# Five changes to the order of work in a hybrid decoder step: query copies, decay tiles, transposes, small loads, first output weights

## The chip, the core and the metric

The kernel runs on one core of a Trainium2 chip. Its engines each work through a queue of their own in order: TensorE (PE: matmuls and transposes; PEld is its weight load), VectorE (DVE), ScalarE (ACT), GpSimd (POOL), and SyncE (SP), which issues nearly all transfers (DMAs). Engines wait for one another by semaphores. The metric is device time in microseconds (us) of one execution, lower is better.

## The reference

One layer of a decoder for a prompt of 1024 tokens (with 16 learned meta tokens ahead of it) and, beside it, 8 sequences that decode 4 tokens each over 1024 cached ones:

```python
h = rms_norm(x, norm_pre_g[l])
(q, k, v), sg, (gq, gk, gv, gf), gg = branch_inputs(h, w_in[l], w_alpha[l], b_alpha[l])
o_sb = sb_prompt(q, k, v, sb_bias[l])
o_gla, s_end = gla_prompt(gq, gk, gv, gf)
x = x + rms_norm(branch_output(o_sb, sg, o_gla, gg, gla_norm_g[l], w_out[l]), norm_post_g[l])
...
log_f = jax.nn.log_sigmoid((ga @ w_alpha + b_alpha).astype(jnp.float32)) / GLA_TAU
...
sp = jnp.where(mask, jax.nn.softplus(z), 0.0)
later = lax.cumsum(sp, axis=z.ndim - 1, reverse=True) - sp
return jnp.where(mask, jnp.exp(jax.nn.log_sigmoid(z) - later), 0.0)
...
S_new = (jnp.exp(b_last[:, :, 0, :])[..., None] * S
         + jnp.einsum('bhsk,bhsv->bhkv', k * jnp.exp(b_last - b), v))
...
mixed = jnp.concatenate([o_sb * jax.nn.silu(sg), o_gla * jax.nn.silu(gg)], axis=-1)
return mixed @ w_out
```

`sb_*` is stick-breaking attention (8 heads of 128), `gla_*` gated linear attention (4 heads, keys of 128, values of 256, chunks of 64). The decoding tokens do the same with keys and values from pages of a cache, found by a page table, and with a stored GLA state. The new keys, values and states are outputs too.

## The kernel before

Everything is f32; each product is made of three matmuls of a high and a low part (`wh`, `wl` of the weights, `hh`, `hl` of the activations). `ident`, `ntri`, `nones` are constant matrices.

An in-projection (`inproj`) makes 128 columns of `h @ w_in` for all 1072 tokens: eight weight blocks of 256 rows (SP loads `wr`, ACT casts it to `wh` in L184, DVE makes `wl` in L185), and for each block three token chunks of up to 384 (`acc_*_0` to `_2`, three PSUM banks) of six matmuls (L289 to L291). After each chunk it calls `W.beat()`. The Weaver `W` holds generators that do all other work: each beat advances those that are due, and `yield n` puts a generator off by n beats. A unit is thus 24 beats. A scheduler then sets each engine's order by priorities and dependences; `urgent()` raises priority for weights and evacuations, and `spread(ins)` ties an instruction's place (without a wait) to the last matmul issued, `W.mark`.

Staging buffers of 128x384 (`stage(...)`, pool `stg`) are seven in rotation.

The stages, one after the other on PE:

- Norms and transposes of x; then eight attention heads. A head projects v, k and q, one unit each. `ev_q` evacuates a query chunk: ACT writes the high part scaled (L620), DVE the low part from PSUM (L621), ACT the sample queries `qsm`. `load_v` reads back the values (`vr`, a DMA) and casts them to V (ACT L483, DVE L484). `attend` runs tiles with their exponentials (X, Y, hi_s; L490, L512) woven into the next head's units.
- `low_rank` (acc_ga, L315), then gates 0 to 2. `gate_group` evacuates a gate chunk: ACT copies `gx` (L438); DVE and ACT turn it into silu in `gs` (DVE L424, ACT L425 and L426, DVE L427, ACT L428, DVE L429); DVE multiplies it with the attention output `go` (L430); SP writes it to `md` in DRAM (L431).
- Four GLA heads: units gk, gq, gv_0, gv_1. `decay` makes the gates' logs (loads `walr` in L720, cast in L731, matmul `al` in L740). `level_masks` makes seven masks. `by_token` transposes keys and values (`tr_k`, `tr_v`, L868, evacuated in L870 and L873); `packed` transposes the sample rows (`trp_k`, `trp_v`, L857) into `pk` and `pv` (ACT L858, DVE L860). All these transposes use one PSUM bank. `chunks` then runs U (L930) and o per pair of chunks. A GLA head waits for its `kd` by `while "kd" not in res: W.beat()`.
- Gates 3 and 4; then gates 5 to 13, with the sample decoding: `z_feed` has made key products of the cached pages all along (`jk`, DVE L384, each fed by a page `kp`, 64 KB, SP), two beats a page, from the first head on. After its last page follow the masked sum `zm` (L1064), `spb` (L1087), `new_keys` (matmul Cs, L1105, and Cn), `chain` for each sequence (scan, matmuls C, L1133 to L1136) and `paged_values` (dO).
- Gates 14 and 15: `load_small` fetches the sample columns of the gates from `md` (L1206).
- The output projection, from seven products of combined 512-column blocks: `weights` loads `wr`, ACT casts into `ring` (L1315), DVE the low part (L1316); `split` makes the forms `f` (L1265); the matmuls are L1452 to L1454 into `b`.

## Time and profile before

| | us |
|---|---|
| median of three runs | 2154.19 (2152.64 to 2156.18) |
| the profiled execution | 2153.79 |
| its span in the trace | 2152.1 |
| PE busy in it | 2078.1 |
| DVE busy | 1572.5 |
| ACT busy | 993.1 |

The granted clock of PE was 0.991 of full speed over the span. Lines of the profile name the engine, the source line (L12 is line 12 of the kernel), the operation and out<-in by the program's names. A timeline row gives start, duration, engine, line and operation, and in brackets how long the engine had been idle and what ended that. In the view of waits a row gives who waited, for whom, how long in all, how often, and the longest.

### The profile page before, as it was taken

To read this page: it belongs to the slowest core of one execution; us is meant where nothing else is said; L and a number is where in the kernel's file an instruction comes from. 1 tells how busy PE (TensorE), PEld (TensorE's weight loads), DVE (VectorE), ACT (ScalarE), POOL (GpSimd) and SP (SyncE) were. 2 spreads that over 40 slices of the span, in tenths; PEclk is the share of its full clock that TensorE was granted. 3 is DMA by queue.
4 is the path that set the end of the run, shared out by engine and by line. 5 is a ranking of instruction groups with operands and counts; after the bars stand their busy time and mean duration, and the time that the engine had idled before them with its cause. 6 is when DMAs were issued, how large, how long until landed. Compare 5 with 4: busy or idle time off the path is not lost.

```text
span 2152.1 us, 43331 instructions
## 1 busy us (share of the span) xinstructions
PE 2078.1 (97%) x12546; PEld 1872.8 (87%) x12546; DVE 1572.5 (73%) x6592; ACT 993.1 (46%) x2536; POOL 83.2 (4%) x298
## 2 busy tenths in 40 slices
PE   5999999999999999999999999999999999999997
PEld 5999999998999979998899898998788887777765
DVE  6368889888898879788788887977544347453575
ACT  7345556564655546432534435343443336332342
POOL 0000010000000010020000000000000000000000
PEclk9999999999999999999999999999999999999999
DMA  6125554554555453442343434335776766452485
GB/s 196 52 70 137 139 158 134 161 146 140 149 152 157 135 142 113 124 100 75 107 106 84 117 80 112 97 83 138 221 228 221 222 200 210 130 158 76 128 277 178
DMA packets 380802, 304.02 MB, mean 141 GB/s; under 512 B 50770, under 2 KB 321042, under 8 KB 380562
## 3 DMA queue, kind: packets, MB, share of 16 engines
q1 hardware_dynamic: 378370, 300.97, 48.0%
q8 instruction: 99, 1.62, 0.3%
q14 instruction: 141, 1.16, 0.2%
q10 hardware_dynamic: 2192, 0.27, 0.1%
HBM read 243.39 MB, written 57.72 MB: 140 GB/s over the span
## 4 chain that ended last, share of the span: by engine, by line
PE 71%; DVE 12%; DMA 10%; ACT 3%; issue 3%; SPq 1%; POOL 0%; DVEq 0%; ACTq 0%; POOLq 0%
DVE jk L384 5%; PE acc_g L289 4%; PE acc_g L291 4%; PE acc_g L290 4%; PE b L1452 4%; PE b L1453 4%; PE b L1454 4%; DMA kp<-in_cache_k_dram 3%; PE acc_k L289 3%; PE acc_k L290 3%; PE acc_k L291 3%; PE acc_gv L289 2%; PE acc_gv L291 2%; PE acc_gv L290 2%; PE acc_q L289 2%
## 5 line engine op out<-in xcount | busy, mean ns | idle before, releaser
L384 DVE SCALAR_TENSOR_TENSOR jk<-kp,qb 128x128 f32<-128x128 f32 x2048 | 590.5, 288 | 90.2 <-DMA kp<-in_cache_k_dram 51.8
L289 PE MATMUL acc_g<-hT,wh_g 128*128 128x304 f32 (+2 forms) x768 | 253.8, 330 | 5.1 <-ACT gx L438 4.7
L291 PE MATMUL acc_g<-hT,wl_g 128*128 128x368 f32 (+2 forms) x768 | 248.0, 323 | 0.0
L290 PE MATMUL acc_g<-hT,wh_g 128*128 128x304 f32 (+2 forms) x768 | 247.9, 323 | 0.0
L289 PEld LDWEIGHTS acc_g<-hT,wh_g 128*128 128x128 f32 x768 | 144.9, 189 | 31.9 <-ACT wh_g L184 12.1
L1452 PE MATMUL b<-ring,f 128*128 128x512 f32 x416 | 165.8, 400 | 3.4 <-ACT b L1351 1.6
L1316 DVE TENSOR_TENSOR ring<-wr,ring 128x512 fp32r<-128x512 f32 x104 | 70.6, 689 | 133.0 <-ACT ring L1315 132.5
L384 DVE DVE_READ_ACCUMULATOR jk<-kp,qb 128x1 f32 x2048 | 166.1, 81 | 0.1
L1453 PE MATMUL b<-ring,f 128*128 128x512 f32 x416 | 162.5, 391 | 0.7 <-DVE ring L1316 0.7
L1454 PE MATMUL b<-ring,f 128*128 128x512 f32 x416 | 162.2, 390 | 0.0
L291 PEld LDWEIGHTS acc_g<-hT,wl_g 128*128 128x128 f32 x768 | 145.0, 189 | 1.6 <-issue 1.6
L290 PEld LDWEIGHTS acc_g<-hT,wh_g 128*128 128x128 f32 x768 | 145.1, 189 | 0.7
L1315 ACT CAST ring<-wr 128x512 fp32r<-128x512 f32 x104 | 64.0, 621 | 162.9 <-DMA wr<-in_w_out_dram 80.9
L512 ACT ACTIVATE X<-X 127x512 f32<-127x512 f32 (+4 forms) x112 | 54.9, 491 | 165.2 <-DVE X L511 165.1
L289 PE MATMUL acc_gv<-hT,wh_gv 128*128 128x384 f32 (+1 forms) x384 | 130.1, 339 | 0.0
L289 PE MATMUL acc_k<-hT,wh_k 128*128 128x378 f32 (+1 forms) x384 | 127.6, 332 | 0.0
L291 PE MATMUL acc_gv<-hT,wl_gv 128*128 128x384 f32 (+1 forms) x384 | 126.0, 328 | 0.0
L289 PE MATMUL acc_q<-hT,wh_q 128*128 128x368 f32 (+2 forms) x384 | 125.4, 326 | 0.0
L290 PE MATMUL acc_k<-hT,wh_k 128*128 128x378 f32 (+1 forms) x384 | 125.4, 326 | 0.0
L291 PE MATMUL acc_k<-hT,wl_k 128*128 128x378 f32 (+1 forms) x384 | 125.2, 326 | 0.0
L290 PE MATMUL acc_gv<-hT,wh_gv 128*128 128x384 f32 (+1 forms) x384 | 125.2, 326 | 0.0
L290 PE MATMUL acc_q<-hT,wh_q 128*128 128x368 f32 (+2 forms) x384 | 123.6, 322 | 0.0
(427 smaller groups left out, 5483.4 us busy)
## 6 DMA issues: line engine op xcount, KB each, us to landing
kp<-in_cache_k_dram SPq DMA_DIRECT2D x512, 64.0 KB
vr<-in_cache_v_dram SPq DMA_DIRECT2D x64, 512.0 KB
qb<-qsd SPq DMA_DIRECT2D x64, 256.0 KB
tf<-in_w_out_dram SPq DMA_DIRECT2D x64, 256.0 KB
td<-tf SPq DMA_DIRECT2D x64, 256.0 KB
wr_g<-in_w_in_dram SPq DMA_DIRECT2D x128, 128.0 KB
wr<-td SPq DMA_DIRECT2D x64, 256.0 KB
wr<-in_w_out_dram SPq DMA_DIRECT2D x48, 256.0 KB
```

The costliest lines, as they stand in the source:

```text
L289: mm(acc[c][:, :n], wh[:, k2, :], hh[k][:, lo:hi], start=(k == 0), stop=False)
L290: mm(acc[c][:, :n], wh[:, k2, :], hl[k][:, lo:hi], start=False, stop=False)
L291: W.mark = mm(acc[c][:, :n], wl[:, k2, :], hh[k][:, lo:hi], start=False, stop=(k == NK - 1)).ins
L384: ins = vec.scalar_tensor_tensor(jk[:], kp[:], 1.0, qbs[h, b][:, t, :], ALU.mult, ALU.mult, accum_out=zt[:, t, NPG - 1 - i:NPG - i])
L512: act.activation(X, X, AF.Exp)
L1315: act.copy(wh, r)
L1316: vec.tensor_tensor(wl, r, wh.bitcast(F32), ALU.subtract)
L1452: mm(bk[:], ah, wh, start=first and k == 0, stop=False, skip_group_check=True)
L1453: mm(bk[:], ah, wl, start=False, stop=False, skip_group_check=True)
L1454: mm(bk[:], al, wh, start=False, stop=last and k == 7, skip_group_check=True)
```

## The change

Line numbers move by 21 to 28: L438 becomes L459, L620 becomes L641 and L646, L857 becomes L881, L860 L884, L868 L892, L930 L955, L1105 L1130.

- Queries: ACT copies each chunk to a staging buffer `qraw`, and a generator splits it from there.
- Decay: `walr` is loaded by one transfer that repeats its rows, for head 0 already during gate 2; the seven masks lie in one tile `lv` in place of seven staging buffers.
- Transposes: the keys' three groups are put two beats apart, `packed` of the keys comes last, and `packed` of the values two beats later.
- `new_keys` waits 16 beats in place of 10, `chain` 10 in place of 8.
- `load_small` is tied to the last matmul issued.
- The first four output weights' casts are tied each to an earlier chunk's matmul: `W.past` keeps the marks, and `spread` takes one from further back.

```diff
+                W.past.append(W.mark)
...
+    def load_ga(g, c):
+        lo, hi = CHUNKS[c]
+        gas[c] = stg.tile([96, 384], F32R, tag="stg", name=f"ga{g}_{c}")
+        nc.sync.dma_start(gas[c][:, :hi - lo].bitcast(F32), gad[:, lo:hi])
+
+    def decay_loads(g):
+        walr[g] = stage(f"walr{g}")[:96, :P]
+        a = w_alpha[0, :, g * P:(g + 1) * P]
+        nc.sync.dma_start(walr[g], bass.AP(tensor=a.tensor, offset=a.offset, ap=[[0, 6]] + [list(d) for d in a.ap]))
+        load_ga(g, 0)
...
-    def spread(ins):
+    def spread(ins, back=0):
         if W.mark is not None:
-            tc.add_manual_dep(ins.ins, W.mark.name, NOSYNC, reason="spread")
+            tc.add_manual_dep(ins.ins, (W.past[-1 - back] if back else W.mark).name, NOSYNC, reason="spread")
...
             def ev_q(c, ps, lo, hi):
                 e = min(hi, REAL)
-                a, b_, n = lo - META, e - META, e - lo
-                act.activation(qt[0][:, a:b_], ps[:, :n], AF.Copy, scale=QSCALE)
-                vec.scalar_tensor_tensor(qt[1][:, a:b_], ps[:, :n], QSCALE, qt[0][:, a:b_].bitcast(F32), ALU.mult, ALU.subtract)
-                if hi > REAL:
-                    act.activation(qsm[:], ps[:, n:], AF.Copy, scale=QSCALE)
-                    W.spawn(sample_q(h, qsm, ks), 5)
+                raw = stage(f"qraw{h}_{c}")
+                act.activation(raw[:, :hi - lo], ps, AF.Copy, scale=QSCALE)
+                W.spawn(split_q(raw, lo - META, e - META, hi - lo))
+
+            def split_q(raw, a, b_, w):
+                n = b_ - a
+                act.copy(qt[0][:, a:b_], raw[:, :n])
+                vec.tensor_tensor(qt[1][:, a:b_], raw[:, :n], qt[0][:, a:b_].bitcast(F32), ALU.subtract)
+                if w > n:
+                    act.copy(qsm[:], raw[:, n:w])
+                    W.spawn(sample_q(h, qsm, ks), 4)
...
         for g in range(3):
+            if g == 2:
+                W.spawn(first_decay_loads(), 14)
             gate_group(g)
...
-            for m in (64, 32, 16, 8, 4, 2, 1):
+            lv = xtile("lv")
+            for i, m in enumerate((64, 32, 16, 8, 4, 2, 1)):
-                a = stage(f"lv{m}")[:, :P]
+                a = lv[:, i * P:(i + 1) * P]
...
-            for i in range(6):
-                nc.sync.dma_start(raw[16 * i:16 * i + 16], w_alpha[0, :, g * P:(g + 1) * P])
+            if g:
+                decay_loads(g)
+            raw = walr.pop(g)
...
+            by_token(kt, kd, (0, 4), col, f"k{g}")
+            yield 2
+            by_token(kt, kd, (4, 4), col, f"k{g}")
+            yield 2
+            by_token(kt, kd, (8, 1), col, f"k{g}")
+            yield 2
             packed(rep_, pk[:], 2, f"k{g}")
-            by_token(kt, kd, (0, 4), col, f"k{g}")
-            yield 1
-            by_token(kt, kd, (4, 4), col, f"k{g}")
-            yield 1
-            by_token(kt, kd, (8, 1), col, f"k{g}")
...
             if c == 2:
+                yield 2
                 packed(rep, pv[:, f * P:(f + 1) * P], 1, f"v{g}_{f}")
...
         def new_keys():
-            yield 10
+            yield 16
...
             ch, cl = split_(s[:].rearrange("p a r -> p r a"), [P, NPG, 32], P, "dc", f"dc{b}")
-            yield 8
+            yield 10
...
-            nc.sync.dma_start(small[c][:, k, :], md[8 * c + k][:, SEQ:TOUT])
+            spread(nc.sync.dma_start(small[c][:, k, :], md[8 * c + k][:, SEQ:TOUT]))
...
-                act.copy(wh, r)
-                vec.tensor_tensor(wl, r, wh.bitcast(F32), ALU.subtract)
+                i = act.copy(wh, r)
+                j = vec.tensor_tensor(wl, r, wh.bitcast(F32), ALU.subtract)
+                if (p, q) == (1, 0) and k < 4:
+                    spread(i, 5 - k)
+                    spread(j, 5 - k)
```

How this moves instructions, at three places. First ACT at the end of the last head's query unit (`acc_q` is the query's accumulator, V the values, `wh_g` a weight of the next unit but one). Before:

```order
L483 CAST V_7_13958<-vr_0_13969 127x384
L544 COPY ost_0_13875<-O_0_13498 128x512
L184 CAST wh_g_1_14440<-wr_g_1_14438 128x256
L483 CAST V_7_13958<-vr_1_14000 127x384
L620 ACTIVATE q_7_13385<-acc_q_0_13388 128x368
L620 ACTIVATE q_7_13385<-acc_q_1_13389 128x384
L184 CAST wh_g_2_14510<-wr_g_2_14508 128x256
L620 ACTIVATE q_7_13385<-acc_q_2_13390 128x272
```

And now:

```order
L641 ACTIVATE qraw_0_13960<-acc_q_0_13430 128x368
L646 CAST q_7_13427<-qraw_0_13960 128x368
L641 ACTIVATE qraw_1_13970<-acc_q_1_13431 128x384
L646 CAST q_7_13427<-qraw_1_13970 128x384
L641 ACTIVATE qraw_2_14000<-acc_q_2_13432 128x304
L184 CAST wh_g_2_14558<-wr_g_2_14556 128x256
L646 CAST q_7_13427<-qraw_2_14000 128x272
L649 COPY qsm_13429<-qraw_2_14000 128x32
L504 CAST V_7_14006<-vr_0_14017 127x384
L533 ACTIVATE X_1_8_14057<-X_1_8_14057 33x32
L504 CAST V_7_14006<-vr_1_14048 127x384
```

The V casts moved from ahead of the query copies to behind them, among the first tiles' exponentials.

Second, ACT after gate 2, whose chunks are `gx_0` to `gx_2`, while PE begins the first GLA unit (`gk`). Before:

```order
L438 COPY gx_0_15982<-acc_g_0_15579 128x368
L425 ACTIVATE gs_16_15986<-gs_16_15986 128x368
L438 COPY gx_1_16001<-acc_g_1_15580 128x384
L426 ACTIVATE gs_16_15986<-gs_16_15986 128x368
L438 COPY gx_2_16039<-acc_g_2_15581 128x304
```

And now:

```order
L459 COPY gx_0_16034<-acc_g_0_15627 128x368
L446 ACTIVATE gs_16_16038<-gs_16_16038 128x368
L459 COPY gx_1_16053<-acc_g_1_15628 128x384
L447 ACTIVATE gs_16_16038<-gs_16_16038 128x368
L184 CAST wh_gk_2_16241<-wr_gk_2_16239 128x256
L446 ACTIVATE gs_384_16076<-gs_384_16076 128x384
L449 ACTIVATE gs_16_16038<-gs_16_16038 128x368
L447 ACTIVATE gs_384_16076<-gs_384_16076 128x384
L459 COPY gx_2_16091<-acc_g_2_15629 128x304
```

The copy of the third chunk moved four places back: its staging buffer is now the first chunk's.

Third, PE in the first GLA head, at the end of its last value unit and the start of the next unit. Before, `trp_k` stood ahead of the keys' transposes:

```order
L857 MATMUL trp_k_18062<-ident,rep_k_17917 96x128
L289 MATMUL acc_gv_1_1_17579<-hT_161,wh_gv_1_7_18047 128x384
L290 MATMUL acc_gv_1_1_17579<-hT_161,wh_gv_1_7_18047 128x384
L291 MATMUL acc_gv_1_1_17579<-hT_161,wl_gv_1_7_18048 128x384
L289 MATMUL acc_gv_1_1_17579<-hT_162,wh_gv_1_7_18047 128x384
L290 MATMUL acc_gv_1_1_17579<-hT_162,wh_gv_1_7_18047 128x384
L291 MATMUL acc_gv_1_1_17579<-hT_162,wl_gv_1_7_18048 128x384
L868 MATMUL tr_k_0_18066<-ident,gk_16075 128x128 x4
```

Now it stands behind the second `trp_v` and the first U:

```order
L881 MATMUL trp_v_1_18208<-ident,rep_v_1_18143 96x128
L289 MATMUL acc_gk_0_18218<-hT_150,wh_gk_1_18292 128x384
L290 MATMUL acc_gk_0_18218<-hT_150,wh_gk_1_18292 128x384
L291 MATMUL acc_gk_0_18218<-hT_150,wl_gk_1_18293 128x384
L955 MATMUL U_0_18304<-gv_0_17100,kd_18097 128x128
L955 MATMUL U_0_18304<-gv_1_17614,kd_18097 128x128
L881 MATMUL trp_k_18212<-ident,rep_k_17954 96x128
```

The DVE step that frees the bank for it, `pv`, stands now behind these rows (before, the split of `wal` came after it):

```order
L405 SCALAR_TENSOR_TENSOR jk_5_6_0_18246,zt_5_18005<-kp_5_6_18161,qb_5_17898 128x128
L405 SCALAR_TENSOR_TENSOR jk_5_6_1_18248,zt_5_18005<-kp_5_6_18161,qb_5_17898 128x128
L185 TENSOR_TENSOR wl_gk_3_18483<-wr_gk_3_18480,wh_gk_3_18482 128x256
L405 SCALAR_TENSOR_TENSOR jk_5_6_2_18250,zt_5_18005<-kp_5_6_18161,qb_5_17898 128x128
L755 TENSOR_TENSOR wal_18383<-walr_18254,wal_18383 32x128
L884 TENSOR_TENSOR pv_17099<-trp_v_1_18208,pv_17099 32x128
```

`trp_k` moved behind `pv`, and `pv` behind one more page of key products (`kp_5_6`) and `wal`.

More of the change, by code (lines that the diff above doesn't have):

```diff
@@ L55, in __init__ @@
     def __init__(self):
-        self.now, self.n, self.live, self.heap, self.mark = 0, 0, 0, [], None
+        self.now, self.n, self.live, self.heap, self.mark, self.past = 0, 0, 0, [], None, []
     def spawn(self, gen, delay=0, lasting=False):
@@ L326, in low_rank, with first_decay_loads @@
                     nc.sync.dma_start(gad[32 * i:32 * i + 32, lo:hi], t[:, :n].bitcast(F32))
+    gas, walr = {}, {}
+    def load_ga(g, c):
[7 more added lines that the diff above has]
+        load_ga(g, 0)
+    def first_decay_loads():
+        decay_loads(0)
+        return
+        yield
     dk_cm = tc.tile_pool(name="dk", bufs=2, side="right")
@@ L618, in ev_q @@
                 e = min(hi, REAL)
-                a, b_, n = lo - META, e - META, e - lo
-                act.activation(qt[0][:, a:b_], ps[:, :n], AF.Copy, scale=QSCALE)
-                vec.scalar_tensor_tensor(qt[1][:, a:b_], ps[:, :n], QSCALE, qt[0][:, a:b_].bitcast(F32), ALU.mult, ALU.subtract)
-                if hi > REAL:
-                    act.activation(qsm[:], ps[:, n:], AF.Copy, scale=QSCALE)
-                    W.spawn(sample_q(h, qsm, ks), 5)
+                raw = stage(f"qraw{h}_{c}")
[8 more added lines that the diff above has]
+                    W.spawn(sample_q(h, qsm, ks), 4)
+                return
+                yield
             inproj(C_SQ + h * P, ev_q, META, f"q{h}")
@@ L716, in decay @@
         def decay(g, cb):
-            raw = stage(f"walr{g}")[:96, :P]
-            for i in range(6):
-                nc.sync.dma_start(raw[16 * i:16 * i + 16], w_alpha[0, :, g * P:(g + 1) * P])
-            gas = {}
-            def load_ga(c):
-                lo, hi = CHUNKS[c]
-                gas[c] = stg.tile([96, 384], F32R, tag="stg", name=f"ga{g}_{c}")
-                nc.sync.dma_start(gas[c][:, :hi - lo].bitcast(F32), gad[:, lo:hi])
-            load_ga(0)
+            if g:
+                decay_loads(g)
+            raw = walr.pop(g)
             yield 6
@@ L737, in decay @@
                 if c < 2:
-                    load_ga(c + 1)
+                    load_ga(g, c + 1)
                 ps = gps.tile([P, 512], F32, tag="P", bufs=2, name=f"al{g}_{c}")
```

## The prediction

> **What bounds the kernel now.** I read the page's busy shares first, then the tensor engine's waits, then the clock in short windows, and last the timeline at each wait that the change touches. TensorE (PE) is busy almost throughout:

> ```profile
> span 2152.1 us, 43331 instructions
> ...
> PE 2078.1 (97%) x12546; PEld 1872.8 (87%) x12546; DVE 1572.5 (73%) x6592; ACT 993.1 (46%) x2536; POOL 83.2 (4%) x298
> ```

> The 74 us in which PE is not busy, and the time in which it runs at half clock, are all that a change of order can win; its matmuls stay. The view of waits says who held PE up (in all, times, longest, in us):

> ```profile
> PE acc_g L289 <- ACT gx L438: 4.7, 2, 2.4
> ...
> PE acc_ga L315 <- DVE q L621: 3.5, 1, 3.5
> PE trp_v L857 <- ACT gv L873: 3.1, 1, 3.1
> ...
> PE tr_k L868 <- DVE pk L860: 3.0, 4, 0.7
> ...
> PE al L740 <- DMA kp<-in_cache_k_dram: 2.7, 1, 2.7
> PE acc_v L289 <- DVE q L621: 2.7, 3, 1.5
> ...
> PE Cs L1105 <- issue: 1.6, 1, 1.6
> ...
> PE b L1452 <- ACT gx L438: 1.0, 2, 0.7
> PE b L1452 <- ACT ring L1315: 0.8, 2, 0.5
> ```

> The windows view adds a price that the waits don't show. Its columns are length, then busy time (with instructions) of PE, PEld, DVE, ACT, POOL, then the granted clock, the DMA share and GB/s:

> ```profile
> 791.00:794.50 3.50, 1.93 (x6) 0.87 (x7) 3.17 (x14) 1.66 (x6) 0.00 (x0) 0.53 0.26 72
> 794.50:798.00 3.50, 3.50 (x16) 2.14 (x15) 2.89 (x18) 1.33 (x6) 0.21 (x1) 0.50 0.80 244
> 798.00:801.50 3.50, 3.50 (x24) 2.33 (x23) 3.06 (x15) 1.03 (x4) 0.00 (x0) 0.99 0.10 27
> ...
> 1511.30:1515.00 3.70, 3.70 (x14) 3.23 (x14) 2.66 (x7) 1.57 (x4) 0.00 (x0) 0.54 0.65 237
> 1515.00:1518.00 3.00, 3.00 (x22) 3.00 (x21) 1.13 (x3) 2.46 (x6) 0.00 (x0) 1.00 0.99 312
> ...
> 1528.00:1531.80 3.80, 2.20 (x12) 1.57 (x11) 2.85 (x6) 1.38 (x2) 0.00 (x0) 1.00 0.78 243
> 1531.80:1535.30 3.50, 3.50 (x15) 1.61 (x15) 0.84 (x2) 1.08 (x2) 0.00 (x0) 0.52 0.34 126
> ```

> After a wait the clock stands near 0.5 for one stretch. At 1531.8 fifteen matmuls take 3.50 us; at the rate of 1515 to 1518 (22 in 3.0) they take 2.05, so the stretch cost 1.45. At 1511.3, 14 take 3.70 in place of 1.91: 1.8. I take 1.4 a stretch, since some of those matmuls are of odd shapes. After 791 there are two stretches: 22 matmuls in 5.43 busy us, which at the rate of 798 to 801.5 (24 in 3.5) take 3.2: 2.2.

> [...]

> **The change, part by part.**

> *Queries.* In each of eight heads ScalarE (ACT) now copies the accumulator out at once, and a split from SBUF follows. Before:

> ```profile
> 790.75 0.51 ACT L483 CAST V<-vr 127x384 fp32r<-127x384 f32 x1 [4.23 <-DMA vr<-out_dram]
> 791.16 0.85 ACT L620 ACTIVATE q<-acc_q 128x368 fp32r<-128x368 f32 x2
> ...
> 791.98 0.53 DVE L621 SCALAR_TENSOR_TENSOR q<-acc_q,q 128x368 fp32r<-128x368 f32 x1
> ```

> ACT stood 4.23 us before a cast that waited for a load, with the query behind it, and PE behind VectorE's (DVE's) half of the query. Now the raw copies come ahead of those casts, and no DVE step lies before the release. Removed: 3.5 + 2.7 + 2.2 of clock = 8.4. Added: 24 copies of some 0.45 us (0.85 for two), on an engine 46% busy: nothing, as long as the V casts behind them don't hold it. Those casts still wait for their loads, now in front of the first attention tiles' exponentials and of a weight cast. The nearest row is the 4.23 us above; PE reaches that weight two blocks of 18 matmuls later, 5.3 us at the rate of 798, so I take 1.4 in all (0 to 4.2). Net -7.0 (-8.4 to -4.2).

> *Decay tiles and masks.* The alpha weights come as one transfer during the third gate unit instead of six later, the masks in one tile. That removes the 2.7 us wait of `al` and one stretch: -4.1. But the two loads hold two of the seven staging buffers, and the copy of the third gate chunk now gets the buffer of the first, which DVE still reads (L429). Rows:

> ```profile
> 906.49 0.40 ACT L438 COPY gx<-acc_g 128x304 f32<-128x304 f32 x1
> ...
> 907.45 0.46 PE L289 MATMUL acc_gk<-hT,wh_gk 128*128 128x304 f32 x1
> ...
> 908.50 0.29 DVE L384 SCALAR_TENSOR_TENSOR jk<-kp,qb 128x128 f32<-128x128 f32 x1 [3.23 <-DMA kp<-in_cache_k_dram]
> ...
> 911.53 0.53 DVE L429 TENSOR_TENSOR gs<-gs,gx 128x368 f32<-128x368 f32 x1
> ...
> 919.84 0.30 ACT L731 CAST wal<-walr 96x128 fp32r<-96x128 f32 x1 [3.33 <-DMA walr<-in_w_alpha_dram]
> ```

> PE uses that bank at 907.45, and DVE frees the buffer at 912.06: with 0.4 for the copy, 5.0 of wait at most. In the new order of SP's queue the page of keys that held DVE 3.23 us no longer stands behind the 256 KB query block, so I take half, +2.5 (0 to 5.0, and 1.4 if the clock falls). Net -1.6 (-4.1 to +2.3).

> *trp_v, 3.1 us and a stretch.* ACT's order there is unchanged; long exponentials of the masks' stage stand ahead of the `gv` copies that PE awaits, and they ran late. The decay work now starts some 50 DVE instructions earlier. Even odds: -2.2 (-4.5 to 0).

> *Transposes spaced*, in four GLA heads:

> ```profile
> 1018.74 0.27 PE L857 MATMUL trp_k<-ident,rep_k 128*96 128x128 f32 x1
> 1020.80 0.66 PE L868 MATMUL tr_k<-ident,gk 128*128 128x128 f32 x4 [0.74 <-DVE pk L860]
> ...
> 1027.52 0.32 PE L857 MATMUL trp_v<-ident,rep_v 128*96 128x128 f32 x1
> ...
> 1028.36 0.61 PE L930 MATMUL U<-gv,kd 128*128 128x128 f32 x4
> ...
> 1027.76 0.29 DVE L384 SCALAR_TENSOR_TENSOR jk<-kp,qb 128x128 f32<-128x128 f32 x1 [2.05 <-DMA kp<-in_cache_k_dram]
> ...
> 1029.10 0.28 DVE L860 TENSOR_TENSOR pv<-trp_v,pv 32x128 fp32r<-32x128 f32 x1
> ...
> 1030.69 0.28 DVE L732 TENSOR_TENSOR wal<-walr,wal 32x128 fp32r<-32x128 f32 x1 [0.98 <-ACT wal L731]
> ```

> All these transposes share one PSUM bank, so each waits until the one before is read. `trp_k` no longer stands before `tr_k`: -3.0. It now follows `trp_v` after three accumulating matmuls and the two U: about 1.1 us (0.84 to U with four, one fewer, and 0.45 for U). But `pv` ended 1.86 us after `trp_v` started, behind a wait for keys; and the split of `wal` and one more group of key products now stand ahead of it in three heads. With an idle DVE nothing is lost; at 1.86 it is 0.8; behind `wal` (1030.97) and `pv`, 2.6. I take 1.2: +4.8 (0 to 10.4). Net +1.8 (-3.0 to +7.4). The longer wait for `kd` adds some five beats without matmuls per head, so the key products run about 20 beats earlier in the program by the fifth gate unit.

> *New keys, chain.* Because of those beats the sample stage starts a gate unit's worth earlier, and Cs stands 20 PE instructions earlier in spite of its longer delay:

> ```profile
> 1510.30 0.41 DVE L1087 TENSOR_TENSOR spb<-spn,bmask 32x256 f32<-32x256 f32 x1
> ...
> 1506.85 0.60 DVE L1064 TENSOR_TENSOR zm<-znall,bmask 32x256 f32<-32x256 f32 x1 [0.82 <-DMA znall<-znd]
> ...
> 1490.92 0.51 ACT L425 ACTIVATE gs<-gs 128x368 f32<-128x368 f32 x1 [3.49 <-DVE gs L424]
> ```

> PE waited 1.6 us for `spb` (1510.30 to 1510.71); now its DVE rows come some three weight blocks ahead. The second chain's C waited 1.6 (3.80 less 2.20 in the window above) and stands 24 matmuls later. Each loses its stretch: 1.6 + 1.4 + 1.6 + 1.4 = -6.0 (to -3.0, if one stays). One of the two acc_g waits (2.3, with 1490.92 as its cause: key products ahead of the gate's DVE step) changes its reason: the products are gone, but the masked sum `zm`, which waits for a transfer, now stands before the next gate step. -1.0 (-2.3 to +2).

> *Small loads, first output weights.* Sixteen small loads go from SP's middle to the gates 14 and 15; ACT's form casts no longer sit in front of the last gate copies. Seven of the loads now stand ahead of the last gate's transfer `go`, where SP had room:

> ```profile
> 1801.81 0.91 SPq L1340 DMA_DIRECT2D gpost<-in_norm_post_g_dram  x2
> 1806.65 0.33 SPq L421 DMA_DIRECT2D go<-od  x1
> ...
> 1498.71 1.41 SPq L1206 DMA_DIRECT2D small<-md  x3
> ```

> Seven at 0.47 are 3.3 us, in a hole of 3.9. If the hole closes, the 3.3 us fall on `go`, ahead of which nothing of PE's waits. Of 1.0 + 0.8 us: -0.8 (-1.8 to +1).

> **Sum.** -7.0 - 1.6 - 2.2 + 1.8 - 6.0 - 1.0 - 0.8 = -16.8. The profiled execution took 2153.79 us, the median of the runs is 2154.19; 2153.8 - 16.8 = 2137.

> **Rivals.**
> Everything wins: -8.4 - 4.1 - 4.5 - 3.0 - 6.0 - 2.3 - 1.8 = -30, 2124. For it: each removed wait has a named cause that the order takes away. Against: DVE is 73% busy, and it stands in all the new waits.
> The new waits take the gain back: the transposes at +7.4, the staging buffer at +2.3, `trp_v` stays, one of Cs and C stays (-3.0), the gate +2, the queries at -7.0: +1.7, 2155. For it: five of them stand behind DVE's key products, which wait for pages.
> The queries' part does nothing, because PE then waits for the copies behind a weight cast: 2144. A smaller relative: the half-clock stretches after the 2.7, 1.6 and 1.6 us waits have another cause and stay, 3 x 1.4 = 4.2 less, 2141. [...]
> Slower: the V casts. ACT stops at each of them until its load lands, and in every head the exponentials and a weight cast stand behind. If PE pays the 4.23 us of the row above in eight heads, that is 33.8 in place of 1.4: 2137 + 32 = 2169. It decides from (16.8 + 4.3 + 1.4) / 8 = 2.8 us a head. Against: the 5.3 us until that weight is needed.

> **How the numbers follow.** Forecast 0.56; everything wins 0.13; queries or clock without effect 0.10; taken back 0.13; slower by the V casts 0.08. A difference under 0.2% (4.3 us) can't be told from none: faster 0.79, same 0.13, slower 0.08. The range 2125 to 2152 leaves out the slower case, half of the taken-back one and a part of the best: under 2 in 10.

> **What would show it.** In the waits of the changed kernel, the rows of PE on q, on `al`, on Cs and on C are gone, and the clock stays near 1 at 791, 921, 1511 and 1532. `tr_k` on `pk` is gone; a row of `trp_k` on `pv` with four waits near 1.2 us is there, and acc_gk on gx with about 2.4 + 2.5. I am wrong if ACT's waits for vr show up again as waits of PE for z, O or weights, or if `trp_k` waits over 3 us.

## The result: slower by 1.6%

The changed kernel took 2186.62 us (median of 6 runs, 2183.01 to 2192.83) where the kernel before took 2153.05 (6 runs, 2149.54 to 2156.18): a ratio of 1.016, interval 1.014 to 1.018. The forecast was 2137, with a range up to 2152. The profiled execution took 2187.82 us, and its page begins:

```profile
span 2186.1 us, 43342 instructions
...
PE 2085.4 (95%) x12546; PEld 1876.3 (86%) x12546; DVE 1573.2 (72%) x6592; ACT 1001.5 (46%) x2560; POOL 79.9 (4%) x298
```

PE is not busy for 2186.1 - 2085.4 = 100.7 us, in place of 74.0: 26.7 of the 34.0 us that the spans differ by are waits. The other 7.3 are busy time, though the matmuls are the same: by the clock's record PE was busy at half clock for 36.1 us in place of 28.7, which makes up for about half of it (3.7 us). The view of PE's waits (us in all, times, longest) says where:

```profile
...
PE acc_g L289 <- ACT gx L459: 8.7, 8, 3.3
PE z L547 <- ACT hi_s L511: 8.2, 8, 2.9
PE z L527 <- DVE q L647: 8.2, 5, 2.9
PE trp_k L881 <- DVE pv L884: 7.9, 4, 3.1
PE acc_g L291 <- DVE wl_g L185: 6.4, 2, 6.1
PE trp_v L881 <- ACT gv L897: 5.9, 3, 2.3
...
PE acc_gk L289 <- ACT gx L459: 4.0, 2, 3.3
...
PE b L1480 <- ACT ring L1340: 2.4, 2, 1.4
PE b L1480 <- ACT b L1379: 1.8, 1, 1.8
PE b L1480 <- ACT gx L459: 1.5, 1, 1.5
```

Most rows that the change was to remove are gone: no wait of acc_v or acc_ga for q, none of `al`, of `tr_k`, of Cs or of C. The wait of trp_v for gv, which had even odds, has grown from 3.1 to 5.9. In their place stand rows that were absent or shorter: z on q and z on hi_s (z is a tile of the attention's scores, made from q; hi_s is ACT's cast of what follows from it), trp_k on pv, the third gate unit on wl_g, and eight waits of the gates for gx in place of two. Two of the rows above stood in the kernel before as

```profile
PE z L526 <- ACT hi_s L490: 3.9, 6, 1.9
...
PE acc_gk L289 <- ACT gx L438: 2.4, 1, 2.4
```

To see which stage lost what, I set the start of the same matmul in both traces side by side. PE's projection matmuls come in one order in all kernels here (but for four of 7920 that change places), so the difference of two starts is the lag up to there, and the difference of two lags is what a stage cost (us against the trace of the kernel before):

| stage, and its end in the trace before | changed | u_query | u_decay | u_transp | u_small | m_vfirst | m_masks | u_keys | m_bank | best1 | best2 | best3 | best4 |
|---|---|---|---|---|---|---|---|---|---|---|---|---|---|
| start, 98 | +1.5 | +1.6 | +0.9 | +0.7 | +0.5 | -0.1 | +0.2 | +1.1 | 0.0 | +0.2 | +0.5 | +0.9 | -0.4 |
| attention, first two gates, 888 | +9.4 | -5.4 | +5.6 | +8.6 | +4.2 | -3.8 | +5.0 | +4.6 | +6.6 | -1.7 | -3.5 | -1.5 | -6.2 |
| third gate, first decay, 968 | +6.9 | +7.8 | -2.0 | +7.3 | +7.6 | +7.0 | +0.5 | +4.8 | +7.6 | 0.0 | +0.2 | -3.5 | +0.4 |
| GLA heads, 1430 | +9.0 | +8.7 | +13.6 | +6.6 | +8.5 | +7.4 | +7.8 | +11.0 | +6.3 | +7.9 | +4.6 | +12.8 | +7.7 |
| sample stage, 1559 | -8.2 | -7.1 | -8.0 | -4.1 | -9.0 | -7.5 | -8.7 | -9.0 | -8.2 | -7.3 | -8.4 | -8.3 | -8.2 |
| gates 5 to 13, 1761 | +6.6 | +6.7 | +8.0 | +5.3 | +5.7 | +4.1 | +5.1 | 0.0 | +5.8 | 0.0 | 0.0 | 0.0 | 0.0 |
| last gates, 1801 | +3.6 | +0.6 | +3.5 | +3.1 | +0.6 | +2.9 | +2.0 | +2.5 | +1.4 | +2.1 | +0.2 | +3.5 | +0.1 |
| output, end | +5.2 | +2.7 | +2.5 | +1.5 | +1.9 | +3.0 | +2.0 | +4.5 | +2.4 | +3.5 | +2.0 | +2.9 | +4.4 |

The other columns are the experiments below. One column is one execution: where the code of a stage is the same, the traces still differ. In the attention stage the seven kernels with the change's queries run from +4.2 to +9.4 (6.3 on average), so a single entry is good to some 3 us, and the timed ratios decide. The kernel before was traced in the first set alone, where its median was 2153.05 us; in the later sets it was 2147.8 to 2148.4. So the columns behind the first are measured against a trace some 5 us longer than the kernel before was in their own set: that of best2 ends 4.3 us ahead, where the times put it 0.7 behind. Those of u_small, m_vfirst, m_masks and m_bank show the shortest of four executions, that of best3 the longest of twelve.

### The profile page after: what moved, and what is told of

It is laid out like the page before. It is cut to its first block, busy times and chain, and to the rows that moved or that the text cites. A ratio compares the mean times of both kernels' runs of the same rounds, so it can differ in the third digit from the quotient of the medians.

```text
span 2186.1 us, 43342 instructions
## 1 busy us (share of the span) xinstructions
PE 2085.4 (95%) x12546; PEld 1876.3 (86%) x12546; DVE 1573.2 (72%) x6592; ACT 1001.5 (46%) x2560; POOL 79.9 (4%) x298
## 4 chain that ended last, share of the span: by engine, by line
PE 65%; DVE 13%; DMA 12%; issue 4%; ACT 4%; SPq 1%; POOL 1%; DVEq 0%; ACTq 0%; POOLq 0%
DVE jk L405 5%; DMA kp<-in_cache_k_dram 4%; PE b L1480 4%; PE acc_g L289 4%; PE b L1481 4%; PE b L1482 4%; PE acc_g L291 3%; PE acc_g L290 3%; PE acc_k L289 3%; PE acc_k L290 3%; PE acc_k L291 3%; PE acc_q L289 2%; PE acc_q L290 2%; PE acc_q L291 2%; PE acc_gv L289 2%
## 5 line engine op out<-in xcount | busy, mean ns | idle before, releaser
L289 PE MATMUL acc_g<-hT,wh_g 128*128 128x368 f32 (+2 forms) x768 | 257.7, 336 | 9.9 <-ACT gx L459 8.7
L290 PE MATMUL acc_g<-hT,wh_g 128*128 128x368 f32 (+2 forms) x768 | 249.8, 325 | 0.0
L289 PEld LDWEIGHTS acc_g<-hT,wh_g 128*128 128x128 f32 x768 | 146.6, 191 | 38.6 <-issue 21.9
L1340 ACT CAST ring<-wr 128x512 fp32r<-128x512 f32 x104 | 64.3, 621 | 162.3 <-DMA wr<-in_w_out_dram 77.3
L289 PE MATMUL acc_gv<-hT,wh_gv 128*128 128x384 f32 (+1 forms) x384 | 130.1, 339 | 0.0
L289 PE MATMUL acc_k<-hT,wh_k 128*128 128x378 f32 (+1 forms) x384 | 127.6, 332 | 0.0
L185 DVE TENSOR_TENSOR wl_g<-wr_g,wh_g 128x256 fp32r<-128x256 f32 x128 | 54.0, 422 | 99.8 <-ACT wh_g L184 95.7
L289 PE MATMUL acc_q<-hT,wh_q 128*128 128x368 f32 (+2 forms) x384 | 125.3, 326 | 0.0
```

The costliest lines, as they stand in the source:

```text
L185: vec.tensor_tensor(wl, raw[:], wh.bitcast(F32), ALU.subtract)
L289: mm(acc[c][:, :n], wh[:, k2, :], hh[k][:, lo:hi], start=(k == 0), stop=False)
L290: mm(acc[c][:, :n], wh[:, k2, :], hl[k][:, lo:hi], start=False, stop=False)
L1340: i = act.copy(wh, r)
```

## Experiments: each part undone

The runs were timed against the kernel before on the same chip, and the ratio is what compares them:

| run | what it is | ratio to the kernel before | interval |
|---|---|---|---|
| changed | the whole change | 1.0160 | 1.0140 to 1.0180 |
| u_query | queries undone | 1.0102 | 1.0080 to 1.0125 |
| u_decay | decay loads and masks undone | 1.0140 | 1.0123 to 1.0157 |
| u_transp | transposes undone | 1.0162 | 1.0140 to 1.0184 |
| u_small | small loads, first output weights undone | 1.0155 | 1.0137 to 1.0173 |
| u_keys | delays of new keys and chain undone | 1.0111 | 1.0091 to 1.0131 |
| m_vfirst | V's loads in their old place | 1.0115 | 1.0096 to 1.0135 |
| m_masks | mask casts later | 1.0133 | 1.0114 to 1.0153 |
| m_bank | small transposes in other banks | 1.0137 | 1.0120 to 1.0155 |
| best1 | five mendings | 1.0041 | 1.0028 to 1.0054 |
| best2 | and decay loads not early | 1.0006 | 0.9995 to 1.0018 |
| best3 | and trp_v in its old bank | 1.0023 | 1.0012 to 1.0033 |
| best4 | best3 with the old queries | 1.0033 | 1.0019 to 1.0047 |

**u_query.**

```diff
-                raw = stage(f"qraw{h}_{c}")
-                act.activation(raw[:, :hi - lo], ps, AF.Copy, scale=QSCALE)
-                W.spawn(split_q(raw, lo - META, e - META, hi - lo))
+                act.activation(qt[0][:, a:b_], ps[:, :n], AF.Copy, scale=QSCALE)
+                vec.scalar_tensor_tensor(qt[1][:, a:b_], ps[:, :n], QSCALE, qt[0][:, a:b_].bitcast(F32), ALU.mult, ALU.subtract)
...
```

> The changed kernel with the queries as before (one ACT step and one DVE step from the accumulator, no raw copy); all else stays changed. The changed kernel took 2186.6; its matmuls of the third gate unit's start ran 10.9 us later than in the kernel before, 1.5 of it from the very start. Theory A: the new split (its DVE half behind other work, its buffers) holds PE's first score product of every head; the 9.4 us go, and with them the PE waits of z on q L647: 2177. Theory B, the prediction's: the query part wins 7.0 us and the 9.4 have another cause: 2194.

2170.15 us, 1.0102: the queries' part costs 0.0058, of 2150 us 12.5. That is theory A, and more than it gave: the attention stage goes from +9.4 to -5.4.

**u_decay.**

```diff
-            if g == 2:
-                W.spawn(first_decay_loads(), 14)
...
-                a = lv[:, i * P:(i + 1) * P]
+                a = stage(f"lv{m}")[:, :P]
...
+            for i in range(6):
+                nc.sync.dma_start(raw[16 * i:16 * i + 16], w_alpha[0, :, g * P:(g + 1) * P])
```

> The changed kernel with the decay loads and the masks as before (six loads issued by the first decay step, each mask in a staging buffer); all else stays changed. Theory A: DVE's seven mask casts wait for POOL mask by mask, and the third gate unit's last weights behind them hold PE 6.1 us and a half-clock stretch; with the staging buffers' 3.3 us all of it goes, and the al wait of about 4 comes back: PE's lag against the kernel before falls by 7 to 10, 2177 to 2180. Theory B, the casts are only where a delay shows that came from the attention stage before: the gap stays elsewhere, 2185 to 2190.

2178.38, 1.0140: 0.002 or 4 us less, between the two, and the intervals overlap. The trace tells where: the third gate and first decay go from +6.9 to -2.0, with the 6.1 us gap gone, but the heads behind them lose 4.6 more. Theory A holds for the place and overstates the sum.

**u_transp.**

```diff
+            packed(rep_, pk[:], 2, f"k{g}")
             by_token(kt, kd, (0, 4), col, f"k{g}")
-            yield 2
+            yield 1
...
-            packed(rep_, pk[:], 2, f"k{g}")
...
-                yield 2
                 packed(rep, pv[:, f * P:(f + 1) * P], 1, f"v{g}_{f}")
```

> The changed kernel with the transposes of the GLA heads in the old order (trp_k first, no spacing); all else stays changed. Theory A: trp_k behind pv costs more than forecast (7.9 us of waits, and trp_v waits 3.6 at two new places), and the beats shift the later gates' copies: the lag of 8.9 us over the GLA heads and up to 6.6 over the gates after them go: 2171 to 2178. Theory B: the transposes cost the 1.8 forecast and the rest of the lag there is DVE's key products wherever they stand: 2185.

2183.62, 1.0162: nothing, as theory B had it, though by cancelling. The heads lose 6.6 in place of 9.0. The sample stage gains 4.1 in place of 8.2, since Cs waits again; PE's waits of this run:

```profile
PE tr_k L891 <- DVE pk L883: 2.9, 4, 0.7
...
PE Cs L1128 <- issue: 1.7, 1, 1.7
```

So it is the transposes' beats that removed the wait for Cs; that of C stays away without them. With the old order the heads still lose 6.6, and trp_v waits four times (8.0 in all). In this run ACT's cast of `wal` stands ahead of the `gv` copies and waits for its load (12.9 us in four times); the changed kernel has the same cast one step further on, ahead of `pv` (11.2 us in four).

**u_small.**

```diff
-            spread(nc.sync.dma_start(small[c][:, k, :], md[8 * c + k][:, SEQ:TOUT]))
+            nc.sync.dma_start(small[c][:, k, :], md[8 * c + k][:, SEQ:TOUT])
...
-                if (p, q) == (1, 0) and k < 4:
-                    spread(i, 5 - k)
-                    spread(j, 5 - k)
```

> The changed kernel with the small loads and the first output weights as before; all else stays changed. Theory A: these loads, now between the last gates' transfers, are what makes gate 14 and the output part 8.8 us later than in the kernel before: 2178. Theory B: the last gates are late because the key products ahead of them stand elsewhere (the transposes' beats), and this part is worth its forecast of 0.8: 2186 to 2188.

2180.74, 1.0155: theory B; the part is worth nothing that can be told. Its last gates stand at +0.6, but so do those of u_query, which has the part.

## Experiments: one cause taken away, the change kept

**m_masks.** The trace of the changed kernel before the gap of 6.1 us, DVE's rows (start, duration, and in brackets how long DVE stood before the row and for whom):

```profile
904.33 0.25 DVE L739 CAST lvl<-lv 128x128 uint8<-128x128 f32 x1 [2.42 <-POOL lv L736]
...
909.29 0.45 DVE L739 CAST lvl<-lv 128x128 uint8<-128x128 f32 x1 [1.32 <-POOL lv L736]
...
913.18 0.23 DVE L739 CAST lvl<-lv 128x128 uint8<-128x128 f32 x1 [1.77 <-POOL lv L736]
...
914.51 0.42 DVE L185 TENSOR_TENSOR wl_g<-wr_g,wh_g 128x256 fp32r<-128x256 f32 x1
```

and the view of the masks' tile:

```profile
L734 POOL TENSOR_SCALAR_AFFINE_SELECT lv<-lv x14: 233/356/653, 903.3 to 911.3; 128x64 f32<-128x64 f32 x14
...
  DVE lvl L739: 7.8, 7
```

POOL's 35 steps for the seven masks take from 901 to 913. DVE has the seven casts in its order there, waits for each (7.8 us in all), and the weight split `wl_g` that PE needs stands behind the last. In the kernel before, the first mask's staging buffer came free only with the gate's last DVE step: POOL stood 24.1 us for it and began at 917, when the third gate's matmuls were done, and DVE waited for a mask once, 1.3 us. By the view of the same tile:

```profile
L701 POOL MEMSET lv<- x7: 199/204/273, 917.1 to 928.6; 128x128 f32 x7
...
  DVE gs L429: 24.1, 1
```

The windows around the gap in the changed kernel (length, busy time of PE, PEld, DVE, ACT, POOL, then the clock) show PE idle and then at half clock:

```profile
908.80:915.00 6.20, 0.07 (x2) 0.02 (x1) 2.96 (x16) 0.03 (x1) 4.34 (x12) 0.88 0.04 12
915.00:918.50 3.50, 3.50 (x11) 3.50 (x12) 3.19 (x22) 0.00 (x0) 0.00 (x0) 0.50 0.31 80
```

The edit ties each cast behind the latest projection matmul; in its trace they start at 930 to 938 us:

```diff
-                vec.tensor_copy(lvl[m][:], a)
+                spread(vec.tensor_copy(lvl[m][:], a))
```

> The changed kernel with one line more: each of the seven mask casts on DVE is tied behind the latest projection matmul, which puts them some 80 DVE rows later, behind POOL's masks; the masks, their tile and the early decay loads stay. Theory A: the casts alone, waiting for POOL, make the gap of 6.1 us and its half-clock stretch before the third gate unit's end: some 11 us go there, the al gain of 4 stays: ratio to the kernel before 1.016 less 0.005, 1.011. Theory B: walr's transfer (ACT's wait of 2.9 us for it) or the staging buffers make the gap: 1.015 to 1.016.

2175.55, 1.0133: 0.0027 or 5.8 us less, and the two intervals overlap a little. In its trace the stage falls from +6.9 to +0.5 and the wait for wl_g is gone; but acc_gk's waits for gx, which the prediction had, are 5.7 us in place of 4.0:

```profile
PE acc_gk L289 <- ACT gx L459: 5.7, 2, 3.1
```

Theory A for the cause, and half its size: a part of acc_gk's waits was hidden behind the gap.

**m_vfirst.** In the changed kernel at the end of the fifth head's queries, ACT and then DVE:

```profile
510.41 0.22 ACT L649 COPY qsm<-qraw 128x32 f32<-128x32 f32 x1
514.75 0.51 ACT L504 CAST V<-vr 127x384 fp32r<-127x384 f32 x1 [4.13 <-DMA vr<-out_dram]
```

```profile
511.45 0.29 DVE L405 SCALAR_TENSOR_TENSOR jk<-kp,qb 128x128 f32<-128x128 f32 x1 [3.67 <-DMA kp<-in_cache_k_dram]
...
511.67 0.54 DVE L647 TENSOR_TENSOR q<-qraw,q 128x368 fp32r<-128x368 f32 x1
...
513.81 0.43 DVE L647 TENSOR_TENSOR q<-qraw,q 128x272 fp32r<-128x272 f32 x1
```

```profile
514.30 0.24 PE L527 MATMUL z<-q,k 128*33 128x32 f32 x1 [2.87 <-DVE q L647]
```

PE waits here 2.9 us for the last of DVE's three steps of the split; the first stands behind a key product that waits 3.67 us for its page, the others behind more key products. And ACT's exponentials stand behind a cast of V that waits 4.13 us for its load. The loads themselves, by the view of their line in a window from 485 to 516, first in the changed kernel, then in u_query:

```profile
L499 SPq DMA_DIRECT2D vr<-out_dram x3: 382/385/415, 511.9 to 516.0; - x3
```

```profile
L499 SPq DMA_DIRECT2D vr<-out_dram x3: 363/377/679, 484.4 to 488.0; - x3
```

They are issued 28 us later, and the lag between the two kernels is only 8 us there. The staging buffers are a ring of seven; the three raw copies now come ahead of V's three in it, so V's loads are ordered behind the raw copies. The edit asks for V's buffers 18 beats into the query unit of 24, ahead of the raw copies:

```diff
-        def values(h):
+        def values(h, wait=0):
...
-            W.spawn(load_v(h, V))
+            W.spawn(load_v(h, V), wait)
...
+            V = values(h, 18)
             inproj(C_SQ + h * P, ev_q, META, f"q{h}")
-            V = values(h)
```

> The changed kernel with the loads of V taken out of the staging ring ahead of the raw query copies (18 beats before the unit's end), so that SP issues them where the kernel before did; raw copies and split stay. Theory A: the raw copies take three of seven staging buffers, V's loads stand some 40 SP rows later for it, and ACT's and DVE's V steps in front of the exponentials are the loss of the attention stage: the lag of the third gate unit's start falls from 5 to 11 us to below 0, ratio about 1.010, as with the queries undone, or 1.008 with the removed query waits. Theory B: the loss is the split's DVE half behind key products that wait for pages, wherever V is: z on q L647 keeps its 8 us, ratio 1.013 to 1.016.

(The 18 beats run from the unit's start, so V's buffers are asked for six beats before its end.)

2171.79, 1.0115: 0.0045 or 9.7 us less, and the attention stage at -3.8 in place of +9.4. V's loads come at 487.6 to 491.6 again. Waits of PE in this run:

```profile
PE z L527 <- DVE q L647: 6.2, 6, 2.3
...
PE z L547 <- ACT hi_s L511: 1.8, 3, 1.4
```

The wait on hi_s falls from 8.2 to 1.8. That on q stays, so theory A holds for the loss and theory B for what is left: the raw copies trade PE's waits for the accumulators (3.5 + 2.7 before) against 6.2 for the split.

**u_keys.** One of the eight waits of the gates, in the changed kernel:

```profile
1596.28 0.68 DVE L1154 TENSOR_TENSOR_SCAN ds<-sm,ds 128x256 f32<-128x256 f32 x1
...
1597.00 0.68 ACT L1079 CAST dc_h<-ds 128x256 fp32r<-128x256 f32 x1 [0.98 <-DVE ds L1154]
...
1597.89 0.47 ACT L459 COPY gx<-acc_g 128x384 f32<-128x384 f32 x1
1598.41 0.19 PEld L289 LDWEIGHTS acc_g<-hT,wh_g 128*128 128x128 f32 x1 [1.38 <-ACT gx L459]
1598.41 0.45 PE L289 MATMUL acc_g<-hT,wh_g 128*128 128x384 f32 x1 [1.07 <-ACT gx L459]
```

A cast of the sample's chain stands on ACT ahead of the gate's copy and waits for DVE's scan. With the longer delays such casts fall onto the gates' ends (acc_g waits 8.7 us for gx, in eight times); the edit takes both delays back, so no run tells the 16 from the 10.

```diff
         def new_keys():
-            yield 16
+            yield 10
...
-            yield 10
+            yield 8
             C = dps.tile([P, 256], F32, tag="C", name=f"C{b}")
```

> The changed kernel with the delays of new keys and of the chain as before (10 and 8 beats); all else stays changed. Theory A: the longer delays removed the waits for Cs and C, about 6 us; they come back: ratio 1.018 to 1.019. Theory B: the shift of the key products by the transposes' beats did that, or the sample work only moved onto the later gates (6.6 us more there): 1.013 to 1.016.

2171.9, 1.0111: 0.0049 or 10.5 us less. The cause is theory B's, and the gain is more than either theory gave: gates 5 to 13 lose nothing any more, the sample stage keeps its gain (-9.0), and neither Cs nor C waits.

```profile
PE acc_g L289 <- ACT gx L459: 3.9, 2, 3.4
```

**m_bank.** The trp_k of the second head, in the changed kernel (ACT, DVE, PE):

```profile
1179.53 0.30 ACT L754 CAST wal<-walr 96x128 fp32r<-96x128 f32 x1 [2.68 <-DMA walr<-in_w_alpha_dram]
1179.74 0.25 ACT L882 CAST pv<-trp_v 96x128 fp32r<-96x128 f32 x1
```

```profile
1180.98 0.28 DVE L884 TENSOR_TENSOR pv<-trp_v,pv 32x128 fp32r<-32x128 f32 x1
```

```profile
1181.32 0.32 PE L881 MATMUL trp_k<-ident,rep_k 128*96 128x128 f32 x1 [3.12 <-DVE pv L884]
```

ACT's cast of `wal` waits 2.68 us for its load with `pv` behind it, DVE reads the bank after more key products, and PE waits for the bank. DVE's part is the greater: in u_decay ACT's cast of `wal` waits in none of these places, and the row stays:

```profile
PE trp_k L879 <- DVE pv L882: 6.8, 4, 2.6
```

```diff
-            ps = gps.tile([P, 512], F32, tag="tr", name=f"trp_{nm}")
+            ps = gps.tile([P, 512], F32, tag="P", bufs=2, name=f"trp_{nm}")
```

> The changed kernel with the small transposes trp_v and trp_k in the two banks that the decay products use, no longer in the one bank that all the transposes share. Theory A: trp_k and trp_v wait only because the bank is read late (DVE's half of pv behind key products, ACT's copies of gv behind the cast of wal, which waits for its load): the waits trp_k on pv (7.9) and trp_v on gv (5.9) go, the lag over the four heads falls from 9 to about 0: ratio 1.016 less 0.004 to 0.006, 1.010 to 1.012. Theory B: PE then waits at U for kd or pv instead, since the late step itself is needed: 1.014 to 1.016.

2177.9, 1.0137: 0.0023 or 5 us less, between the theories, and the intervals overlap. trp_k no longer waits, but the transposes now stand earlier and trp_v waits for the masks' products in the new banks and for its own input:

```profile
PE trp_v L881 <- DVE at L832: 6.6, 4, 2.1
...
PE trp_v L881 <- DVE rep_v L875: 3.2, 3, 2.3
```

## Experiments: the mendings together

**best1** is the edits of m_vfirst, m_masks, u_keys and m_bank, and `spread(...)` around ACT's and DVE's step for `wal`.

> The changed kernel with five mendings: V's loads ahead of the raw query copies, mask casts tied behind the projection, delays of 10 and 8 beats as before, the small transposes in the other banks, the casts of wal tied behind the projection. By the lags of the single runs: attention -3, third gate unit and al 0, GLA heads 0 to +5, sample part -9, gates 5 to 13 0, last gate and output +3 to +6: -9 to +1 in all, ratio 0.996 to 1.001. If the gains don't add, because every delay taken away uncovers another: 1.003 to 1.008.

2157.82, 1.0041: inside the second forecast. The four gains timed alone sum to 0.0144, and 0.0119 came. Attention -1.7, third gate 0.0, gates 5 to 13 0.0; the GLA heads still cost 7.9.

**best2.**

```diff
-            if g == 2:
-                W.spawn(first_decay_loads(), 14)
...
-            if g:
-                decay_loads(g)
+            decay_loads(g)
```

> As the run before, but the first decay loads are issued by the decay step again, as one transfer, and no longer during the third gate unit. The two staging buffers are free for the gate copies: the wait of acc_gk on gx (3 to 6 us) goes; al may wait again (2.7 and a half-clock stretch, 4). If the buffers are the dearer, 2 to 3 us less than the run before; if al is, 1 to 2 more.

2149.15 against 2148.43, 1.0006 (0.9995 to 1.0018): 0.0035 or 7.5 us less than best1. acc_gk waits once, 2.6 us in place of 4.7 in best1 (2.4 in the kernel before), and `al` 0.4. So the early loads were dearer than late ones, by the times. That it is their buffers is not shown: acc_gq now waits 2.0 us, the stage stands at +0.2 against 0.0, and the rest of the 7.5 us isn't located. With this run the loss is accounted for in sum: the whole change but for these mendings stands within 0.2% of the kernel before. Two of the mendings, the other banks and the tie of `wal`, are not in the kernel before, so a part may be made up for and not undone; the tie was never timed alone. The five steps (0.0045 for V, 0.0027 masks, 0.0049 delays, 0.0023 banks, 0.0035 early loads) sum to 0.0179, and the two kernels lie 0.0154 apart.

**best3** puts trp_v back into the shared bank.

```diff
+            if lo == 2:
+                ps = gps.tile([P, 512], F32, tag="P", bufs=2, name=f"trp_{nm}")
+            else:
+                ps = gps.tile([P, 512], F32, tag="tr", name=f"trp_{nm}")
```

> As the run best2, but only trp_k goes to the decay products' banks and trp_v stays in the shared one, behind gv. In best2 the trp_v of the second half waited 2.1, 0.4 and 0.4 us for its own rep_v, and those of the first half 1.1, 0.6, 1.9 and 1.6 for the masks' products, which hold those banks. If both came from the bank, 4 to 7 us go: ratio 0.997 to 0.999. If the first half's waits go back to ACT's gv copies, and only the second half's go: 0.999 to 1.000.

2152.24, 1.0023 (best2 1.0006, and the intervals overlap): neither; no gain, and trp_v waits for ACT's gv copies again (8.3 in 4). Its profiled execution was the longest of its twelve (2148.26 to 2160.68), so its column in the table overstates it.

**best4** is best3 with the queries of u_query.

> As the run best3, but with the queries as in the kernel before (no raw copies, V's loads where they were). Theory A: with V's loads in place the raw copies only trade PE's waits for the accumulators against waits for the split, and nothing is between this run and best3 (within 0.15%). Theory B: the copies are worth their forecast of 7 us: this run is 0.3% above best3.

2153.8, 1.0033 against 1.0023: theory A. Once V's loads stand in their old place, the raw copies gain nothing that can be told. No version here beats the kernel before.

## Why the prediction was wrong, step by step

Undone one by one, the five parts are worth 0.0130 of the 0.0160: queries 0.0058, decay 0.0020, transposes -0.0002, small loads 0.0005, delays 0.0049.

**Queries, -7.0: about +12.5.** What it removed is right: the waits for q at the accumulators are gone, and where the old kernel ran at half clock behind the last of them (0.50 from 794.5 to 798), the windows of the changed kernel read 1.00:

```profile
796.50:800.00 3.50, 3.50 (x23) 3.38 (x22) 2.57 (x16) 1.84 (x4) 0.00 (x0) 1.00 0.54 178
800.00:803.50 3.50, 3.01 (x20) 1.97 (x18) 3.36 (x18) 2.19 (x7) 0.41 (x1) 1.00 0.70 217
```

The step that failed is "nothing, as long as the V casts behind them don't hold it", with 1.4 for the V casts. I counted the copies' time on ACT and not their buffers, though I counted the same ring for the decay loads in the next paragraph. The rival "Slower: the V casts" had the mechanism, at 33.8 us, and got 0.08; m_vfirst shows 9.7 us for it. What it missed is why: the loads themselves are issued later. The second miss is that the split's DVE half, left without a price because no release of a bank waits for it, stands behind key products that wait for pages: PE waits 6.2 to 8.2 us for it.

**Decay tiles and masks, -1.6: about +4,** with overlapping intervals. The removed `al` is right. The buffer wait of "+2.5 (0 to 5.0)" is there: acc_gk on gx, 2.4 before, is 4.0, and 5.7 in m_masks. Issuing the loads late again is worth 7.5 by best1 and best2, more than that wait. The step that failed is one that isn't there: the masks were costed at nothing, with no cover named. Their own tile frees POOL of its wait for a buffer, so that the masks start at 901 and DVE's casts stand in front of the third gate's last weights. The old trace had the rows for it, POOL's 24.1 us of wait and its masks from 917 to 933; I read DVE's and SP's queues and not POOL's. It measured 5.8 alone.

**trp_v, -2.2: not removed.** Three waits (5.9) in place of one (3.1). "ACT's order there is unchanged" holds. What the prediction hoped for didn't come. In the first head ACT's exponentials, ahead of the `gv` copies, still wait for DVE's step X (2.57 us, 3.20 before), and in the third, where they hadn't waited, they do now. Before, and in the changed kernel:

```profile
1256.09 1.09 ACT L792 ACTIVATE X<-X 128x1056 f32<-128x1056 f32 x1
```

```profile
1279.85 1.09 ACT L815 ACTIVATE X<-X 128x1056 f32<-128x1056 f32 x1 [2.48 <-DVE X L814]
```

So "The decay work now starts some 50 DVE instructions earlier" won little in the first head (trp_v's wait there is 2.3 in place of 3.1) and nothing in the others; what delays X there no run shows.

**Transposes, +1.8: 0 in all.** The wait of trp_k measured 7.9 against 4.8, inside the bounds of 0 to 10.4; tr_k's 3.0 went. The beats, which the prediction saw, gave the sample stage's gain, which it booked under the next item. That the total lies near the forecast is luck: a larger cost and a gain booked elsewhere cancel.

**New keys and chain, -6.0: the waits went, and the delays cost 10.5.** "Because of those beats the sample stage starts a gate unit's worth earlier" was the right cause: u_keys has neither wait without the longer delays, and u_transp, with the delays and without the beats, has Cs again (C's wait is gone in both). The step that failed is the price of the delays themselves, which stood at nothing with no cover named: what they do to the chains behind them, whose casts then stand on ACT ahead of the gate copies, wasn't asked.

**The gate at 1490, -1.0,** is right in sign, 2.28 before to 0.53. **Small loads and output weights, -0.8:** nothing was found; the two waits it was to shorten, b on gx and on the ring, rose from 1.0 and 0.8 to 1.5 and 2.4.

**The clock.** The three stretches of half clock that the prediction took away (at 921, 1511 and 1532) are gone with their waits: in the changed kernel the clock is 1.00 around `al`, which starts at 940.66, and no stretch of half clock begins between 1012.5 and 1804.4. "Each loses its stretch" is no rule even so, see below.

The range failed with the sum: every item had its own bounds, and none had an upper bound for a thing not thought of. The warning was there, "five of them stand behind DVE's key products, which wait for pages", and got 0.13. Both signs of being wrong that it named appeared: behind V's casts z waits 8.2 us for hi_s in place of 3.9, and trp_k waits up to 3.1.

What stays open: the GLA heads cost 4.6 to 13.6 us in every variant, with old or new transposes. Much of it are PE's waits at the small transposes: those of trp_k, trp_v and tr_k sum to 13.8 us in the changed kernel, 10.9 in u_transp and best1 and 8.0 in best2, against 6.1 before. What makes them late in all variants no run settles. The load of `wal` as one transfer, for which ACT waits 11.2 us in four times, against 3.9 in two before, can't be all of it: with the old loads (u_decay) the heads cost 13.6, and in best1, where no cast of `wal` waits, 7.9. The 1.5 to 5 us in the output part are as large as the differences between traces.

## What to carry over

A tile taken from a shared ring of staging buffers moves every later user of the ring, loads included (here V's loads, by 28 us): count the ring's turn before counting the copy. Before a step is costed at nothing, read the queue of the engine that feeds it, also when that engine is idle 96% of the time. And a delay put in to give work time has to be taken out and timed alone, since something else may have done the job already.

## What the clock did

The prediction priced a stretch of half clock for waits from 1.6 us on. The traces say otherwise. A wait of 1.8 us at 337.1 in the changed kernel was followed by one; a wait of 3.0 us in u_small was not (windows: length, PE, PEld, DVE, ACT, POOL, clock):

```profile
337.00:339.00 2.00, 0.22 (x2) 0.10 (x1) 1.97 (x8) 1.85 (x5) 0.65 (x2) 1.00 0.16 46
340.10:343.50 3.40, 3.40 (x13) 3.20 (x12) 3.26 (x16) 2.94 (x6) 0.29 (x1) 0.50 0.48 140
```

```profile
1794.40:1797.40 3.00, 0.03 (x1) 0.00 (x0) 2.88 (x6) 0.90 (x3) 0.00 (x0) 1.00 0.68 222
1797.50:1801.00 3.50, 3.50 (x22) 3.47 (x23) 2.89 (x8) 3.08 (x8) 0.00 (x0) 1.00 0.83 258
```
